# Decoder trunk on one core: another order of steps in the two MLPs

## The chip, the cores and the metric

The kernel runs on one core of one Trainium2 chip. The metric is the device time in microseconds of one execution, and the median of several runs is compared. TensorE is called PE below, VectorE DVE, ScalarE ACT, GpSimd POOL, and SyncE SP, as the profile names them.

## What is computed

The reference is a causal decoder trunk of two layers on 256 tokens with a width of 2048, all in float32. Each layer adds an attention mixer and then a dense MLP with a hidden width of 8192. The change touches the MLPs alone:

```python
for layer in range(DEPTH):                       # 2 layers
    h = rmsnorm(x, ln_mix[layer])
    x = x + (even_mixer if layer % 2 == 0 else odd_mixer)(h, ...)
    h = rmsnorm(x, ln_mlp[layer])
    x = x + jnp.square(jax.nn.relu(h @ w1)) @ w2  # w1 2048x8192, w2 8192x2048
return rmsnorm(x, ln_final)
```

## The kernel before

Everything in float32 is made of two halves in PE's float32r type: a high half (a cast by ACT, `wh`) and a low half (what the cast left, a subtraction by DVE, `wl`), and a product takes two or three matmuls of halves. `split` (L149 to L151) makes one pair.

The work of an MLP is one list of steps, `order`, written by the kernel itself and kept as it stands on every engine (the scheduler is off in there). The hidden width is cut into 16 units of 512 columns, and the units into six chunks of 2, 3, 3, 3, 3 and 2 units.

- An **up step** (class `Up`) multiplies two 128-row blocks of `w1` with the transposed input. Eight of them make a unit in four PSUM banks; at the last, `leave` (L746) takes the banks out: four copies by ACT, four additions by DVE, then Relu and Square by ACT. There are four such banks in all, so the next unit's first step needs the additions done. Later `build` turns a unit into the halves that the down steps read: `ah` (ACT) and `al` (DVE) of its values, and of four differences.
- A **down step** multiplies a unit with rows of `w2`. In chunks 0 to 4 two kinds alternate: `Seven` (L848) does a 2x2 block product in seven products instead of eight, for which DVE first adds up four sums `T` (three additions, `sums`) and then ACT and DVE split the weights and the sums into `sh` and `sl` (`split`); `Eight` is the plain product. At a block's last step, `Eight.end` puts the results together (six DVE operations) and queues two additions into `x`. The last chunk has plain steps only.
- `downs(c)` gives a chunk's down steps in four blocks of 512 output columns; `woven` (L960) puts the up steps of chunk c+1 between the down steps of chunk c.
- Most halves are made by ACT and DVE, but some up steps are "moved" (`Up.early`, L785): ACT casts the high half `mh` and writes its negative to `ml`, and a DMA issued by POOL adds the raw weights to `ml` on the way, so that DVE does nothing for them. Here these are the steps i = 1, 4 and 7 of a unit's eight.

Step names used from here on: U2.1.7 is the up step i = 7 of unit 1 of chunk 2, and a star marks a moved one (U2.1.7*); S1.b2.0 and E1.b2.1 are the Seven and the Eight at places 0 and 1 of block 2 of chunk 1's down steps; P5.b0.0 is a plain one of the last chunk.

The loop over the list (L1017) sets how far ahead each engine's part stands in that engine's queue. At place p it emits, in this order: the load for p+7 (SP; six raw buffers), `split` for p+2, `early` for p+4, `sums` for p+3, then the matmuls of p, what ends it (`leave` or `Eight.end`), and one piece of the queue `later` (parts of `build`, additions into `x`):

```python
for p in range(-7, len(order)):
    at(p + 7).load()
    at(p + 2).split()
    at(p + 4).early()
    at(p + 3).sums()
    ...
    at(p).product()
    at(p).end()
    queue_units(p + 1)
    if later:
        later.popleft()[1]()
```

Between the first chunk's up steps and the rest stands one call, `begin` (L976): it ends the input's norm (thirteen small DVE operations) and builds both units of chunk 0 at once.

Of the kernel before, what the change touches and what calls it, by code (L numbers as in the profile page):

```python
# [23 lines left out]
KT = D // P  # L24
# [42 lines left out]
def decoder_trunk(ctx, tc, const, x_in, ln_mix, ln_mlp, ln_final, e_w_in, e_g_q, e_g_kv, e_w_uq, e_w_ukv, e_w_out,  # L67
# [52 lines left out]
    def tick(rate=1):  # L120
        for _ in range(min(rate, len(pend))):
            pend.popleft()()
# [4 lines left out]
    def flush():  # L127
        tick(len(pend))
# [150 lines left out]
    def finish_norm(ss):  # L279
        tot = small.tile([P, NT], F32, name=nm("tot"), tag="tot", bufs=2)  # L280
        r = small.tile([P, NT], F32, name=nm("r"))
        nc.vector.tensor_reduce(tot, ss, axis=AX.X, op=ALU.add)
        rsqrt(r, tot, NT, D)
        return r
# [425 lines left out]
    def mlp(layer, ss, done, tail=None):  # L710
# [3 lines left out]
        with ExitStack() as st:  # L714
# [228 lines left out]
            units = [[Unit(c, n) for n in range(m)] for c, m in enumerate(CHUNKS)]  # L943
            last = len(CHUNKS) - 1

            def ups(c, moved):
                return [Up(u, i, moved and i % 3 == 1) for u in units[c] for i in range(KT // 2)]

            def downs(c):


                seq = []
                for n in range(4):
                    block = {}
                    cs = slice(n * 512, n * 512 + 512)
                    seq.append([Eight(block, i, units[c], cs, c, False) if i % 2 else Seven(block, i, units[c], cs, c)
                                for i in range(2 * CHUNKS[c])])
                return seq

            def woven(a, blocks):  # L960

                out, n = [], len(blocks)
                for j, b in enumerate(blocks):
                    part = a[len(a) * j // n : len(a) * (j + 1) // n]
                    rest, i = part[2:], 0
                    out += part[:2]
                    for k, s in enumerate(b):
                        out.append(s)
                        while i < len(rest) and i * len(b) < (k + 1) * len(rest):
                            out.append(rest[i])  # L970
                            i += 1
                return out

            order = ups(0, False)

            def begin():  # L976
                flush()
                r = finish_norm(ss)
                nc.vector.tensor_mul(rr, r, r)
                for u in units[0]:  # L980
                    u.ready = False
                    for part in u.build():
                        part()

            order.append(Call(begin))
            for c in range(last):
                order += woven(ups(c + 1, True), downs(c))
            blocks = [slice(n * 512, n * 512 + 512) for n in range(4)]
            if tail:
                blocks[3] = slice(1536, 1792)  # L990
# [5 lines left out]

            def queue_units(p):

                for c in range(1, last + 1):
                    for u in units[c]:  # L1000
                        if u.ready and p >= free[c - 1].get(u.n, 0):
                            u.ready = False
                            later.extend((u, part) for part in u.build())


            free, use = [{} for _ in CHUNKS], {}
            for p, s in enumerate(order):
                if isinstance(s, (Plain, Seven)):
                    u = s.units[s.i // 2]
# [3 lines left out]
            if tail:  # L1013
                cs, k0 = slice(1792, 2048), 4 * sum(CHUNKS[:last])
                ends = [Last(j, k0 + 4 * j, cs, j % 2 == 0) for j in range(CHUNKS[last])]
                order += ends
            for p in range(-7, len(order)):  # L1017
                at = lambda q: order[q] if 0 <= q < len(order) else Call(None)
                at(p + 7).load()
                at(p + 2).split()  # L1020
                at(p + 4).early()
                at(p + 3).sums()
                if p < 0:
                    continue
                while p in need and any(u is need[p] for u, _ in later):
# [6 lines that stand above are left out]
                tick()  # L1032
# [10 lines left out]
    ss = even_mixer(new_ss())  # L1043
    ss2 = new_ss()
    mlp(0, ss, lambda n, cs: pend.extend(norm_block(1, n, ss2)))
    ss = odd_mixer(ss2)

# [22 lines left out]
    def leave(t, cs):  # L1070
# [14 lines left out]
        for h in range(0, D, 512):  # L1085
            nc.sync.dma_start(ov[t][:, h : h + 512], xt[:, h : h + 512])

    mlp(1, ss, both, leave)


# [25 lines left out]
```

## Time and profile before

| what | us |
|---|---|
| median of 3 runs (lowest to highest) | 2281.58 (2280.48 to 2284.74) |
| the profiled execution's own time | 2283.93 |
| its span, first to last instruction | 2282.2 |
| PE busy in that span | 2216.2 (97%) |
| DVE busy | 1601.7 (70%) |
| ACT busy | 1245.5 (55%) |
| the two MLPs in the span | 399.8 to 1142 and 1533 to 2263 |

All durations come from the profiled execution. Its PE waits are listed by what released them, and its timeline gives each instruction's start, its length and the idle time before it.

### The profile page before, as it was taken

The page shows a single profiled execution, that of the slowest core. Times are in us where ns is not written, and L with a number is a line of the kernel's source. Part 1 is how long each engine was busy: PE and PEld are TensorE (multiplying, and loading weights), DVE is VectorE, ACT ScalarE, POOL GpSimd, SP SyncE. Part 2 cuts the span into 40 slices and gives each one's busy share as a digit, 9 for nine tenths or more (in the row PEclk, how much of TensorE's full clock was granted, in tenths as well). Part 3 has the DMA queues.
Part 4 walks back from the last instruction along what each step waited for, and adds up shares of the span by engine and source line. Part 5 has one row for each costly group of instructions (what it writes and reads, how often), then busy time and mean ns, then how long its engine had stood idle before and what let it go on. Part 6 is the DMA issues. An engine that isn't in the chain of part 4 may idle for free.

```text
span 2282.2 us, 33668 instructions
## 1 busy us (share of the span) xinstructions
PE 2216.2 (97%) x13086; PEld 1947.4 (85%) x13086; DVE 1601.7 (70%) x2481; ACT 1245.5 (55%) x1659; POOL 72.6 (3%) x88
## 2 busy tenths in 40 slices
PE   8999999999999999999999999998999999999998
PEld 7899988788888888888799999887888888888886
DVE  6767655566778787787665566556667777876786
ACT  6454545555656556555544444455556565556553
POOL 0000000000000000000000000000000000000000
PEclk9999999999999999999999999999999999999999
DMA  7655545578777778677565555455878777786764
GB/s 246 177 164 148 158 157 172 169 219 230 216 205 227 217 219 237 204 216 221 165 192 168 172 170 175 166 175 164 232 213 235 209 223 219 212 250 192 222 203 148
DMA packets 225692, 451.42 MB, mean 198 GB/s; under 512 B 16182, under 2 KB 21244, under 8 KB 225532
## 3 DMA queue, kind: packets, MB, share of 16 engines
q1 hardware_dynamic: 213436, 405.23, 55.8%
q0 software_dynamic: 12096, 44.05, 10.7%
q8 instruction: 102, 1.67, 0.3%
q14 instruction: 58, 0.48, 0.1%
HBM read 403.08 MB, written 2.10 MB: 178 GB/s over the span
## 4 chain that ended last, share of the span: by engine, by line
PE 75%; DVE 10%; issue 6%; DMA 6%; ACT 3%; SPq 0%; DVEq 0%; POOLq 0%
PE bank L185 17%; PE bank L186 16%; PE bank L184 16%; PE bank L809 14%; PE bank L810 7%; DMA ml<-raw 3%; DVE wl L151 3%; DMA raw<-in_mlp_w_dram 2%; DVE sl L151 2%; PE pt L223 1%; ACT wh L150 1%; PE ps L445 1%; DVE x L914 1%; DVE al L151 1%; ACT ah L150 1%
## 5 line engine op out<-in xcount | busy, mean ns | idle before, releaser
L151 DVE TENSOR_TENSOR wl<-raw,wh 128x1024 fp32r<-128x1024 f32 (+3 forms) x554 | 665.7, 1211 | 389.1 <-ACT wh L150 381.1
L150 ACT CAST wh<-raw 128x1024 fp32r<-128x1024 f32 (+3 forms) x554 | 568.6, 1037 | 387.8 <-PE bank L186 162.8
L809 PE MATMUL bank<-xx,wh 128*128 128x512 f32 x1376 | 493.1, 398 | 6.6 <-DVE a L751 6.6
L810 PE MATMUL bank<-xx,wl 128*128 128x256 f32 x1376 | 387.6, 282 | 0.0
L809 PEld LDWEIGHTS bank<-xx,wh 128*128 128x128 f32 x1376 | 260.1, 189 | 67.3 <-DVE a L751 7.6
L810 PEld LDWEIGHTS bank<-xx,wl 128*128 128x128 f32 x1376 | 260.8, 190 | 4.0 <-DVE wl L151 1.6
L184 PE MATMUL bank<-sh,ah 128*128 128x256 f32 (+1 forms) x856 | 250.2, 292 | 13.6 <-ACT sh L150 13.6
L185 PE MATMUL bank<-sl,ah 128*128 128x256 f32 (+1 forms) x856 | 251.7, 294 | 8.4 <-DVE sl L151 8.0
L150 ACT CAST sh<-T 128x1024 fp32r<-128x1024 f32 x112 | 117.8, 1052 | 241.4 <-DVE T L867 241.1
L186 PE MATMUL bank<-sh,al 128*128 128x256 f32 (+1 forms) x856 | 249.4, 291 | 0.0
L809 PE MATMUL bank<-xx,mh 128*128 128x512 f32 x672 | 243.4, 398 | 0.0
L185 PE MATMUL bank<-xx,wh 128*128 128x256 f32 x768 | 216.5, 282 | 0.0
L184 PE MATMUL bank<-xx,wh 128*128 128x256 f32 x768 | 216.3, 282 | 0.0
L186 PE MATMUL bank<-xx,wl 128*128 128x256 f32 x768 | 215.6, 282 | 0.0
L810 PE MATMUL bank<-xx,ml 128*128 128x256 f32 x672 | 192.4, 286 | 17.0 <-DMA ml<-raw 16.9
L185 PE MATMUL bank<-wl,ah 128*128 128x512 f32 (+1 forms) x520 | 204.6, 393 | 1.4 <-DVE wl L151 1.4
L184 PE MATMUL bank<-wh,ah 128*128 128x512 f32 (+1 forms) x520 | 204.4, 393 | 0.0
L186 PE MATMUL bank<-wh,al 128*128 128x512 f32 (+1 forms) x520 | 203.5, 391 | 0.0
L184 PEld LDWEIGHTS bank<-sh,ah 128*128 128x128 f32 x856 | 164.8, 193 | 22.1 <-ACT sh L150 14.8
L185 PEld LDWEIGHTS bank<-sl,ah 128*128 128x128 f32 x856 | 164.6, 192 | 15.8 <-DVE sl L151 13.4
L186 PEld LDWEIGHTS bank<-sh,al 128*128 128x128 f32 x856 | 165.0, 193 | 2.2
L809 PEld LDWEIGHTS bank<-xx,mh 128*128 128x128 f32 x672 | 127.8, 190 | 28.5
(192 smaller groups left out, 3899.1 us busy)
## 6 DMA issues: line engine op xcount, KB each, us to landing
raw<-in_mlp_w_dram SPq DMA_DIRECT2D x510, 512.0 KB, 4.9
raw<-in_o_w_in_dram SPq DMA_DIRECT2D x96, 512.0 KB, 4.1
ml<-raw POOLq DMA_DIRECT2D x84, 512.0 KB, 7.0
raw<-in_e_w_in_dram SPq DMA_DIRECT2D x71, 512.0 KB, 3.6
raw<-in_e_w_out_dram SPq DMA_DIRECT2D x32, 512.0 KB, 3.6
raw<-in_o_w_out_dram SPq DMA_DIRECT2D x32, 512.0 KB, 3.6
raw<-in_e_w_uq_dram SPq DMA_DIRECT2D x8, 384.0 KB, 3.2
raw<-in_e_w_in_dram SPq DMA_DIRECT2D x8, 320.0 KB, 3.9
```

The costliest lines, as they stand in the source:

```text
L150: nc.scalar.copy(hi, raw)
L151: on.tensor_tensor(lo, raw, hi.bitcast(F32), op=ALU.subtract)
L184: nc.tensor.matmul(o, ah, bh, start=first, stop=False, **kw)
L185: nc.tensor.matmul(o, ah, bl, start=False, stop=False, **kw)
L186: nc.tensor.matmul(o, al, bh, start=False, stop=last, **kw)
L223: nc.tensor.transpose(o, src, ident[: src.shape[0], : src.shape[0]])
L445: nc.tensor.matmul(o, q[:, h, t * P : t * P + P], k[:, h, : SPAN[t][1]], start=True, stop=True)
L809: nc.tensor.matmul(u.o[f], wh[:, kk, fs], xx[:, k], start=k == 0, stop=False, skip_group_check=True)
L810: nc.tensor.matmul(u.o[f][:, 0, :], wl[:, kk, fs], xx[:, k, 0], start=False, stop=k == KT - 1, skip_group_check=True)
L914: nc.vector.scalar_tensor_tensor(x[:, t, cs], o, rr[:, t : t + 1], x[:, t, cs], op0=ALU.mult, op1=ALU.add)
```

## The change

It does four things. (1) `begin` is moved four up steps on: the list now goes from the first chunk straight to U1.0.0, U1.0.1, U1.0.2*, then `begin`, U1.0.3 and only then S0.b0.0; `begin` no longer builds the units, which go through the queue `later` like all others. (2) In `woven`, where a unit's first step would stand after a single down step, it is swapped with the next down step, so that two down steps stand between units; it looks only within one chunk's weave. (3) The halves of a Seven are emitted three places ahead instead of two, and the sums four instead of three; `early` comes ahead of the splits. (4) Moved are the steps i = 2 and 5 of eight, instead of 1, 4 and 7: 56 transfers by POOL instead of 84.

```diff
--- before.py
+++ after.py
@@ -944,7 +944,7 @@
             last = len(CHUNKS) - 1
 
             def ups(c, moved):
-                return [Up(u, i, moved and i % 3 == 1) for u in units[c] for i in range(KT // 2)]
+                return [Up(u, i, moved and i % 3 == 2) for u in units[c] for i in range(KT // 2)]
 
             def downs(c):
 
@@ -957,18 +957,23 @@
                                 for i in range(2 * CHUNKS[c])])
                 return seq
 
-            def woven(a, blocks):
+            def woven(a, blocks, lead=2):
 
                 out, n = [], len(blocks)
                 for j, b in enumerate(blocks):
                     part = a[len(a) * j // n : len(a) * (j + 1) // n]
-                    rest, i = part[2:], 0
-                    out += part[:2]
+                    rest, i = part[lead:], 0
+                    out += part[:lead]
+                    lead = 2
                     for k, s in enumerate(b):
                         out.append(s)
                         while i < len(rest) and i * len(b) < (k + 1) * len(rest):
                             out.append(rest[i])
                             i += 1
+
+                for k in range(2, len(out) - 1):
+                    if isinstance(out[k], Up) and out[k].i == 0 and isinstance(out[k - 2], Up) and not isinstance(out[k + 1], Up):
+                        out[k : k + 2] = out[k + 1], out[k]
                 return out
 
             order = ups(0, False)
@@ -977,14 +982,10 @@
                 flush()
                 r = finish_norm(ss)
                 nc.vector.tensor_mul(rr, r, r)
-                for u in units[0]:
-                    u.ready = False
-                    for part in u.build():
-                        part()
-
-            order.append(Call(begin))
+
             for c in range(last):
-                order += woven(ups(c + 1, True), downs(c))
+                order += woven(ups(c + 1, True), downs(c), 2 if c else 4)
+            order.insert(len(units[0]) * KT // 2 + 3, Call(begin))
             blocks = [slice(n * 512, n * 512 + 512) for n in range(4)]
             if tail:
                 blocks[3] = slice(1536, 1792)
@@ -996,9 +997,9 @@
 
             def queue_units(p):
 
-                for c in range(1, last + 1):
+                for c in range(last + 1):
                     for u in units[c]:
-                        if u.ready and p >= free[c - 1].get(u.n, 0):
+                        if u.ready and p >= (free[c - 1].get(u.n, 0) if c else 0):
                             u.ready = False
                             later.extend((u, part) for part in u.build())
 
@@ -1014,12 +1015,14 @@
                 cs, k0 = slice(1792, 2048), 4 * sum(CHUNKS[:last])
                 ends = [Last(j, k0 + 4 * j, cs, j % 2 == 0) for j in range(CHUNKS[last])]
                 order += ends
-            for p in range(-7, len(order)):
+            for p in range(-8, len(order)):
                 at = lambda q: order[q] if 0 <= q < len(order) else Call(None)
                 at(p + 7).load()
-                at(p + 2).split()
                 at(p + 4).early()
-                at(p + 3).sums()
+                for ahead in (2, 3):
+                    if isinstance(at(p + ahead), Seven) == (ahead == 3):
+                        at(p + ahead).split()
+                at(p + 4).sums()
                 if p < 0:
                     continue
                 while p in need and any(u is need[p] for u, _ in later):
```

What this does to the queues at three places follows; the numbers behind a name tell buffers apart.

The first is ACT's queue at `begin` of the first MLP. Ahead of it stand the four copies of unit U0.1 (`a_795` before, `a_800` now); `a_767` is U0.0. Before:

```order
L752 ACTIVATE a_795_4380<-a_795_4380 128x1024
L753 ACTIVATE a_795_4380<-a_795_4380 128x1024
L150 CAST ah_803_4416<-a_767_4190 128x1024
L150 CAST ah_803_4416<-s_805_4420 128x512
L150 CAST ah_806_4426<-a_795_4380 128x1024
L150 CAST ah_806_4426<-s_808_4430 128x512
L150 CAST sh_810_4438<-raw_783_4291 128x768
L150 CAST sh_810_4438<-T_797_4393 128x1024
```

And now:

```order
L752 ACTIVATE a_800_4394<-a_800_4394 128x1024
L753 ACTIVATE a_800_4394<-a_800_4394 128x1024
L150 CAST ah_801_4405<-a_800_4394 128x1024
L150 CAST ah_801_4405<-s_808_4431 128x512
L150 CAST wh_812_4461<-raw_789_4323 128x1024
L150 CAST sh_814_4465<-raw_792_4345 128x768
L150 CAST sh_814_4465<-T_810_4435 128x1024
L150 CAST wh_823_4510<-raw_797_4372 128x1024
```

U0.0 is built eight steps earlier now; only U0.1 is left, and between its second cast and the halves of S0.b0.0 (`sh_814`) stands the high half of U1.0.3 (`wh_812`).

The second is DVE's queue at the passage from chunk 1 to chunk 2, that is from U1.2.7 to U2.0.0, behind the last combination of E0.b3.3 (L909, L914). Before:

```order
L909 TENSOR_TENSOR v_974_5452<-bank_949_5279,v_974_5452 128x512
L914 SCALAR_TENSOR_TENSOR x_74<-v_974_5452,rr_725_3969,x_74 128x512
L865 TENSOR_TENSOR T_977_5464<-raw_959_5351 128x512
L866 TENSOR_TENSOR T_977_5464<-T_977_5464,raw_959_5351 128x256
L867 TENSOR_TENSOR T_977_5464<-T_977_5464,raw_959_5351 128x256
L751 TENSOR_TENSOR a_978_5484<-bank_924_5148,a_978_5484 128x256
```

And now:

```order
L909 TENSOR_TENSOR v_973_5448<-bank_952_5285,v_973_5448 128x512
L914 SCALAR_TENSOR_TENSOR x_74<-v_973_5448,rr_725_3969,x_74 128x512
L151 TENSOR_TENSOR wl_979_5466<-raw_956_5331,wh_978_5465 128x1024
L151 TENSOR_TENSOR sl_981_5470<-raw_959_5349,sh_980_5469 128x768
L151 TENSOR_TENSOR sl_981_5470<-T_972_5432,sh_980_5469 128x1024
L751 TENSOR_TENSOR a_982_5491<-bank_930_5178,a_982_5491 128x256
```

Ahead of U1.2's additions (L751) stood the three sums of S1.b0.0; now these stand ahead of the combination, and the low half of U2.0.1 (`wl_979`) and both low halves of S1.b0.0 (`sl_981`) have come in their place.

The third is ACT's queue at the passage from chunk 2 to chunk 3, behind the last copy of unit U2.2. Before:

```order
L752 ACTIVATE a_1181_6750<-a_1181_6750 128x1024
L753 ACTIVATE a_1181_6750<-a_1181_6750 128x1024
L903 COPY v_1184_6779<-bank_1143_6509 128x256
L150 CAST sh_1187_6791<-raw_1166_6648 128x768
L150 CAST sh_1187_6791<-T_1183_6763 128x1024
```

And now:

```order
L752 ACTIVATE a_1180_6743<-a_1180_6743 128x1024
L753 ACTIVATE a_1180_6743<-a_1180_6743 128x1024
L789 CAST mh_1182_6756<-raw_1169_6662 128x1024
L790 ACTIVATE ml_1183_6757<-mh_1182_6756 128x1024
L150 CAST wh_1184_6761<-raw_1161_6607 128x1024
```

The two operations for U3.0.2* (`mh_1182`, `ml_1183`) now stand behind Relu and Square of U2.2, and the high half of U3.0.1 (`wh_1184`), which was a moved step before, stands behind them; the matmuls of U3.0.1 come two places later in PE's queue than those of E1.b3.5, with U3.0.0 between.

## Rows read from the trace of the kernel before

**Rows 1.** Page, part 1: busy time and share of the span, by engine.
```profile
PE 2216.2 (97%) x13086; PEld 1947.4 (85%) x13086; DVE 1601.7 (70%) x2481; ACT 1245.5 (55%) x1659; POOL 72.6 (3%) x88
```

**Rows 2.** Waits of PE: line <- releaser: us in total, times, longest us.
```profile
PE bank L810 <- DMA ml<-raw: 16.9, 13, 2.3
PE bank L184 <- ACT sh L150: 13.6, 2, 6.8
PE bank L185 <- DVE sl L151: 8.0, 16, 1.0
PE bank L809 <- DVE a L751: 6.6, 2, 3.3
...
PE bank L185 <- DVE wl L151: 1.9, 6, 0.5
```

**Rows 3.** Timeline, PE at `begin`: start us, us, engine, line, operation [idle before].
```profile
448.48 0.39 PE L809 MATMUL bank<-xx,mh 128*128 128x512 f32 x1
...
458.25 0.58 PE L184 MATMUL bank<-sh,ah 128*128 128x256 f32 x1 [6.78 <-ACT sh L150]
...
463.91 0.39 PE L809 MATMUL bank<-xx,wh 128*128 128x512 f32 x1
```

**Rows 4.** Timeline, ACT and then DVE at `begin`.
```profile
448.78 1.03 ACT L150 CAST ah<-a 128x1024 fp32r<-128x1024 f32 x1
453.00 0.62 ACT L150 CAST ah<-s 128x512 fp32r<-128x512 f32 x1 [3.19 <-DVE s L770]
...
460.32 3.49 DVE L151 TENSOR_TENSOR wl<-raw,wh 128x1024 fp32r<-128x1024 f32 x3
463.73 0.69 DVE L865 TENSOR_TENSOR T<-raw 128x512 f32<-128x512 f32 x1
...
465.25 0.95 DVE L151 TENSOR_TENSOR sl<-raw,sh 128x768 fp32r<-128x768 f32 x1
```

**Rows 5.** Timeline, PE and DVE at the passage from U1.2.7* to U2.0.0.
```profile
569.33 0.79 PE L809 MATMUL bank<-xx,wh 128*128 128x512 f32 x1 [3.32 <-DVE a L751]
573.75 0.40 PE L809 MATMUL bank<-xx,mh 128*128 128x512 f32 x1
...
568.86 1.41 DVE L751 TENSOR_TENSOR a<-bank,a 128x256 f32<-128x256 f32 x4
```

**Rows 6.** Timeline, PE, DVE and ACT at the passage from U2.2.7* to U3.0.1*.
```profile
704.84 0.39 PE L809 MATMUL bank<-xx,wh 128*128 128x512 f32 x1
707.64 0.39 PE L809 MATMUL bank<-xx,mh 128*128 128x512 f32 x1
709.44 0.39 PE L810 MATMUL bank<-xx,ml 128*128 128x256 f32 x1 [1.41 <-DMA ml<-raw]
...
686.89 1.23 DVE L151 TENSOR_TENSOR al<-a,ah 128x1024 fp32r<-128x1024 f32 x1 [4.24 <-ACT ah L150]
...
702.29 1.41 DVE L751 TENSOR_TENSOR a<-bank,a 128x256 f32<-128x256 f32 x4
...
703.74 1.06 ACT L752 ACTIVATE a<-a 128x1024 f32<-128x1024 f32 x1 [1.12 <-DVE a L751]
```

**Rows 7.** Timeline, PE and ACT after U2.1.7*, whose last matmul is the row before 653.57.
```profile
653.57 0.28 PE L184 MATMUL bank<-sh,ah 128*128 128x256 f32 x1
...
656.08 0.39 PE L184 MATMUL bank<-wh,ah 128*128 128x512 f32 x1
...
654.63 1.06 ACT L752 ACTIVATE a<-a 128x1024 f32<-128x1024 f32 x1 [0.49 <-DVE a L751]
...
659.67 0.81 ACT L150 CAST sh<-raw 128x768 fp32r<-128x768 f32 x1
```

**Rows 8.** Stretches: us, busy by engine, PEclk (granted clock), DMA share, GB/s.
```profile
979.34:981.50 2.16, 0.38 (x3) 0.07 (x1) 2.06 (x5) 2.16 (x4) 0.00 (x0) 1.00 0.86 283
981.54:985.70 4.16, 4.16 (x15) 3.56 (x16) 4.16 (x6) 1.55 (x2) 0.00 (x0) 0.59 0.74 235
```

**Rows 9.** Tile `ml`: from issue to landing of its 84 transfers.
```profile
DMA to landing us min/median/max: 4.8/7.0/11.2
```

## The prediction

> **What bounds the kernel now.** The page's first part comes first: PE is busy for 2216.2 us, 97% of the span [rows 1]. The change adds no matmul and takes none away; it only puts them in another order. So the time can only move by what PE waits for and by its clock. The second view is PE's list of waits [rows 2]: transfers into `ml` 16.9 us in 13 waits, ACT's `sh` 13.6 in 2, DVE's `sl` 8.0 in 16, DVE's `a` (the banks of a unit not yet taken out) 6.6 in 2, DVE's `wl` 1.9 in 6. All lie in the two MLPs, which repeat each other place by place; together 47.0. Two things add to it. An idle is counted from a matmul's modelled end: in U3.0.1* the second matmul starts 1.80 after the first [rows 6], where it is free to start after 0.23 (an up step of 2.80 us is eight pairs of 512 and 256 columns, so 0.35 a pair and two thirds of it for the first); that is 1.57 lost for an idle of 1.41, 0.16 more, and 6 for the 39 waits. And after the longer waits PE goes on at half its clock: S0.b0.0 takes 463.91 - 458.25 = 5.66 us [rows 3], against 2.51 for S1.b2.2 [rows 7], of which 0.6 are two of the `sl` waits and 2.5 the clock; U2.0.0 takes 4.42 against 2.80, so 1.6 [rows 5]; and behind a wait that left PE 0.38 busy of 2.16 the granted clock is 0.59 of full speed for 4.16 us, so 4.16 x 0.41 = 1.7 [rows 8]. That is 5.8 an MLP, 11.6 in all. The whole of what PE loses in the MLPs is then 47 + 6 + 12 = 65 us. This is all that an order can win; of it one `sl` wait per MLP of 1.0, in the last chunk, is at a place that the change leaves as it is. What may vanish or come back is 63.
>
> **At `begin`.** U1.0.1* begins at 448.48 and is done 2.80 later, at 451.28; S0.b0.0 begins at 458.25 [rows 3]. These 7.0 and the 3.1 of the slow step are 10.1 an MLP. Now U0.0 is built eight steps earlier, beside up steps in which ACT and DVE have room, and PE has U1.0.2* and U1.0.3 to do, until 456.9. But U1.0.3 has to be halved, and its high half stands behind U0.1's second cast on ACT (first order rows). Step by step: `ah` ends at 449.81 [rows 4]; DVE makes `al` (1.14: three low halves in a row take 463.73 - 460.32 = 3.41), the sums `s` (half as many columns as `T`, which takes 465.25 - 463.73 = 1.52; so about 0.9 with their starts) and `T`, until 453.4; the second cast 0.6; the high half of U1.0.3 about 1.0, until 455.1; its low half 1.14, until 456.25. U1.0.3 is due at 454.08, so its second matmul comes 456.25 - 0.23 - 454.08 = 1.9 late. The thirteen small operations of the norm come behind the halves of S0.b0.0 and delay nothing that is due. I add a fall of the clock, 1.7, because two idles of about 1.0 with one matmul between them come nearest to the 1.8 of [rows 8]. Now 3.6, before 10.1.
>
> **Where a moved step stands behind a unit's end.** After U2.1.7*, Relu starts 1.06 after the last matmul, and the fifth operation after that is under way until 659.67, 6.1 after the unit's end [rows 7]. In the changed order five such operations stand between a unit's end and the high half of an up step in two kinds of place, because the moved step is now i = 2 and its `mh` and `ml` are emitted ahead of the halves of i = 0 or 1. The first is U1.2.0, two down steps behind U1.1.7: due 2.51 + 2.80 = 5.3 after the unit's end, high half there after 6.2, low half after 7.35; 1.8 late, and 1.7 for the clock as above: 3.5, new.
>
> The second is each passage from a chunk to the next from chunk 2 on (U2.2 to U3.0, U3.2 to U4.0, U4.2 to U5.0; third order rows), and there DVE is late as well. From 686.89, where PE's freeing of `ah` lets it begin, DVE works through to the additions of U2.2 at 702.29 [rows 6]. Ahead of them there is now one low half more, U2.2.7 being no longer moved (1.14), and the sums of S2.b0.0, emitted a step earlier (1.52): 704.95. The first bank is free 0.4 later, U3.0.0 was due at 704.84: 0.5 late. Relu starts 1.45 after the additions' start, as before (703.74 against 702.29), at 706.4; the high half of U3.0.1 ends 5.1 later, 711.5, the low half at 712.7; its second matmul was due at 705.35 + 2.80 + 0.23 = 708.4: 4.3 late. With the clock, 1.7, this is 6.5 a passage, 19.5 an MLP. Before, a passage lost a wait for `ml` of 1.4 to 2.3 [rows 2, 6].
>
> **At the first passage,** U1.2.7 to U2.0.0, the swap of (2) does not reach: the two steps stand in different weaves, and still side by side. The additions of U1.2 start at 568.86 because the combination of E0.b3.3 and three sums stand ahead of them, and U2.0.0 waits until 569.33 [rows 5]. The sums go (1.52), `wl` of U2.0.1 and both `sl` of S1.b0.0 come (1.14 + 0.95 + 1.14, second order rows): 1.7 later; and since the sums now stand ahead of the combination, that starts up to 0.4 later too. So 3.5 + 2.1 = 5.6, and for the clock 2.0, between the 1.6 after an idle of 3.3 and the 2.5 after 6.8: 7.6; before 5.1.
>
> **Inside a chunk** (after U2.1.7 and its like in three chunks) the waits for `sl` and `ml` go: only one high half and the `sh` pair stand behind Square now, U2.2.1 is halved 4 us ahead of its use, and U2.2.2* has its transfer issued some 8 us ahead, against 7.0 in the median [rows 9]. I count nothing there, and 0.9 at E4.b2.1, whose low half falls behind a combination and three sums (3.1 + 1.3 + 1.5 of DVE work under two steps). Of the 28 transfers less, ACT loses 28 casts and DVE gains 28 subtractions (28 x 1.14 = 32 us over both MLPs): paid where it stands in the sums above, elsewhere covered by the 30% of the span in which DVE is free [rows 1].
>
> **A transfer's price** decides how much more can come. On the rows, `ml` lands 4.8 to 11.2 us after its issue. At a passage it is now issued at about 711 and needed at about 719.4: 7.0 is in time, 11.2 would be 2.8 late. I take the median, so nothing. The Trainium skill, in "DMA: Bandwidth & Descriptors", section "Anatomy of one DMA — SWDGE (gpsimd) path", fits 2.0 us plus the bytes at 436 GB/s, an estimate of 3.2 us for these 512 KB: by that no `ml` would ever be late and the sum would stay as it is. The smallest landing here is 4.8, so the trace does not agree, and the rows decide.
>
> **The sum.** New: 3.6 + 3.5 + 7.6 + 19.5 + 0.9 = 35.1 an MLP, 70 in both, against 63 that go: 7 us slower. The profiled execution took 2283.93 (span 2282.2), so 2291 like it; it lies 2.4 above the median of the runs, and against that median I say 2289.
>
> **Rivals.**
> - *The passages cost no more than U1.2.0.* If DVE catches up ahead of them (its row at 686.89 had been idle for 4.24), the additions start with the unit's end, and a passage costs 1.8, at full clock or not: 3 x 4.7 less an MLP, 28 in all, so 2261. It decides at one point: whether U2.2's additions end before about 703 instead of 706.4. For it: a shift of ACT's or DVE's start by little moves the rest. Against: from 686.89 on the list leaves DVE no gap but two of 0.7. Half of this gives 2275.
> - *The clock stays up* where I charge it for two short idles (`begin`, U1.2.0): 2 x 3.4 = 7 less, 2282, no change. The row with 1.41 idle shows a full clock, that with 1.8 a fall; mine lie at the edge.
> - *Transfers land late*, as at U3.0.1* before (about 10 us after issue): 1.7 at each passage and about 2 after each unit inside a chunk, 11 an MLP: 2311. Three loads at a time ran there; fewer transfers in all speak against it.
> - *The change does less than it says:* this is so for the swap at the passages, seen in the order, and is in the sum.
>
> Chances: the forecast 0.37 (its own range 2283 to 2296), passages cheap 0.24, clock up 0.25, transfers late 0.14. A measurement of this kernel can tell 0.2%, 4.6 us, from no change. Faster 0.25, within 0.28, slower 0.47. The range takes in half of the cheap passages and half of the late transfers: 2264 to 2303.
>
> **What would show it.** Right: PE's waits for `sh` gone (13.6), a wait of about 1.0 before `wh` and `wl` in U1.0.3, `a` waits up from 6.6 to some 14 in 8 places, and `wh` (ACT) waits of about 3.3 in six places, at U3.0.1, U4.0.1 and U5.0.1; granted clock below 0.7 behind these. Wrong: additions of U2.2 that end within 1.5 us of U2.2.7's last matmul, or `ml` waits that remain above 5 us in all.

## The result and the profile after

| what | before | the change |
|---|---|---|
| median, us | 2281.03 (4 runs, 2280.20 to 2284.74) | 2297.01 (4 runs, 2294.80 to 2298.64) |
| ratio, 95% interval | | 1.0066 (1.0049 to 1.0084) |
| the profiled execution's own time, and its span | 2283.93, 2282.2 | 2297.91, 2296.1 |
| mean granted clock of the profiled execution | 0.993 | 0.987 |

The change is slower, by 16 us between the medians and 11 to 19 by the interval. The forecast was 2289 and slower, with a range from 2264 to 2303. Part 1 of the page after, to be held against [rows 1]:

```profile
PE 2230.3 (97%) x13086; PEld 1957.1 (85%) x13086; DVE 1629.7 (71%) x2509; ACT 1215.9 (53%) x1631; POOL 48.5 (2%) x60
```

PE runs the same 13086 matmuls and is busy 14.1 us longer (2230.3 against 2216.2), in a span that is 13.9 longer. PE's waits after say what that means:

```profile
PE bank L809 <- ACT wh L150: 21.7, 10, 3.1
PE bank L809 <- DVE a L751: 13.8, 8, 5.3
PE bank L810 <- DVE wl L151: 8.5, 12, 0.8
...
PE bank L185 <- DVE sl L151: 1.9, 2, 0.9
...
PE bank L185 <- DVE wl L151: 0.7, 3, 0.3
PE bank L810 <- DMA ml<-raw: 0.6, 1, 0.6
```

They come to 47.2 us in 36 waits, against 47.0 in 39 in [rows 2]. The change has not lengthened PE's idle: it took away the waits for `sh` and nearly all those for `ml` and `sl`, and put waits for `wh`, `a` and `wl` of the same sum in their place. But after the new waits PE goes on at half its clock more often. In the MLPs before, the granted clock is 0.50 in six stretches (`begin`, U2.0.0 and U5.0.1* of each), with 22.9 us of matmuls in them; after, in eleven (U1.0.3, U2.0.0, U3.0.1, U4.0.1 and U5.0.1 of each, and U1.2.0 of the first), with 48.6. Matmuls take twice as long there (0.79 us against 0.40 in [rows 5]), so half of that time is lost, and half of the difference is 12.9 of the 14.1 us: nearly the whole loss is slower matmuls.

A table by place follows. A step's loss is the time from its first matmul's start to the next step's, less 2.81 us for an up step, 2.80 for an Eight and 2.52 for a Seven, the lengths of undisturbed ones; a wait ahead of a step's first matmul counts with the step before. Only losses over 0.15 are summed, and the first two steps of each MLP (0.8) and its last chunk, the same in both kernels, are left out. Both MLPs together:

| place | before | after |
|---|---|---|
| `begin` (U1.0.1 to S0.b0.0) | 20.2 | 7.5, and 1.8 at U0.1.2 |
| U1.2.0 | 0 | 5.6 |
| first passage, U1.2.7 to U2.0.0 | 10.2 | 15.9 and 0.3 |
| the three other passages | 13.8 | 42.6 |
| inside chunks 1 to 3 | 17.4 | 1.1 |
| inside chunk 4 | 2.7 | 3.1 |
| sum | 64.3 | 77.8 |

The difference, 13.5, is nearly the span's 13.9. The change gains 27 us, 10.9 at `begin` and 16.3 inside chunks 1 to 3; the passages take back 35, U1.2.0 another 5.6.

**`begin`.** The timeline after, PE, then ACT, then DVE, beside [rows 3, 4]:

```profile
457.00 0.49 PE L809 MATMUL bank<-xx,wh 128*128 128x512 f32 x1 [0.97 <-ACT wh L150]
458.26 0.39 PE L810 MATMUL bank<-xx,wl 128*128 128x256 f32 x1 [0.77 <-DVE wl L151]
...
450.66 1.05 ACT L150 CAST ah<-a 128x1024 fp32r<-128x1024 f32 x1
455.38 0.62 ACT L150 CAST ah<-s 128x512 fp32r<-128x512 f32 x1 [3.68 <-DVE s L770]
455.91 1.04 ACT L150 CAST wh<-raw 128x1024 fp32r<-128x1024 f32 x1
...
456.98 1.23 DVE L151 TENSOR_TENSOR wl<-raw,wh 128x1024 fp32r<-128x1024 f32 x1 [0.25 <-ACT wh L150]
```

U1.0.3's high half stands behind U0.1's second cast, as the order said; the two idles are 0.97 and 0.77, and the place loses 3.8 where 10.1 were lost.

**U1.2.0 and the first passage,** PE at both and DVE at the second, beside [rows 5]:

```profile
529.15 0.50 PE L809 MATMUL bank<-xx,wh 128*128 128x512 f32 x1 [0.75 <-ACT wh L150]
530.41 0.39 PE L810 MATMUL bank<-xx,wl 128*128 128x256 f32 x1 [0.76 <-DVE wl L151]
...
570.47 0.80 PE L809 MATMUL bank<-xx,wh 128*128 128x512 f32 x1 [5.34 <-DVE a L751]
...
568.86 1.22 DVE L151 TENSOR_TENSOR sl<-T,sh 128x1024 fp32r<-128x1024 f32 x1
570.00 1.41 DVE L751 TENSOR_TENSOR a<-bank,a 128x256 f32<-128x256 f32 x4
```

U2.0.0 waits 5.34 instead of 3.32 for the additions, which stand right behind S1.b0.0's low halves.

**A passage**, U2.2.7 to U3.0.1, beside [rows 6]: PE, then DVE, then ACT.

```profile
705.00 0.50 PE L809 MATMUL bank<-xx,wh 128*128 128x512 f32 x1 [0.53 <-DVE a L751]
711.13 0.49 PE L809 MATMUL bank<-xx,wh 128*128 128x512 f32 x1 [3.05 <-ACT wh L150]
712.39 0.58 PE L810 MATMUL bank<-xx,wl 128*128 128x256 f32 x1 [0.77 <-DVE wl L151]
...
701.87 1.23 DVE L151 TENSOR_TENSOR wl<-raw,wh 128x1024 fp32r<-128x1024 f32 x1 [0.26 <-ACT wh L150]
703.01 0.68 DVE L865 TENSOR_TENSOR T<-raw 128x512 f32<-128x512 f32 x1
...
704.53 1.41 DVE L751 TENSOR_TENSOR a<-bank,a 128x256 f32<-128x256 f32 x4
...
705.98 1.06 ACT L752 ACTIVATE a<-a 128x1024 f32<-128x1024 f32 x1 [3.06 <-DVE a L751]
...
708.03 1.03 ACT L789 CAST mh<-raw 128x1024 fp32r<-128x1024 f32 x1
709.09 1.06 ACT L790 ACTIVATE ml<-mh 128x1024 fp32r<-128x1024 f32 x1
710.05 1.03 ACT L150 CAST wh<-raw 128x1024 fp32r<-128x1024 f32 x1
```

Read it from the middle: DVE makes a low half and the sums `T` before it takes unit U2.2 out at 704.53; so Relu starts at 705.98, ACT had been idle for 3.06 until then; behind Square come `mh` and `ml` of U3.0.2*, and only then the high half that U3.0.1 waits for. PE is idle 0.53, 3.05 and 0.77. The clock shows by stretch: U3.0.0 and the idle behind it, U3.0.1, and U5.0.1 of the same MLP (columns as in [rows 8]):

```profile
705.00:711.10 6.10, 3.08 (x16) 2.44 (x16) 0.94 (x3) 5.06 (x6) 0.66 (x1) 1.00 0.16 61
711.10:716.40 5.30, 4.50 (x16) 3.68 (x17) 5.12 (x8) 5.30 (x7) 0.20 (x1) 0.68 0.88 181
...
987.90:994.10 6.20, 5.33 (x16) 4.34 (x17) 5.94 (x9) 4.63 (x7) 0.28 (x1) 0.55 0.90 228
```

The clock is full up to the idle and falls when PE goes on. Transfers into `ml` land 4.5 to 6.8 us after their issue, against 4.8 to 11.2 in [rows 9]:

```profile
DMA to landing us min/median/max: 4.5/5.7/6.8
```

### The profile page after: what moved, and what is told of

The parts are those of the page before. It is cut to its first block, busy times and chain, and to the rows that moved or that the text cites. A ratio compares the mean times of both kernels' runs of the same rounds, so it can differ in the third digit from the quotient of the medians.

```text
span 2296.1 us, 33636 instructions
## 1 busy us (share of the span) xinstructions
PE 2230.3 (97%) x13086; PEld 1957.1 (85%) x13086; DVE 1629.7 (71%) x2509; ACT 1215.9 (53%) x1631; POOL 48.5 (2%) x60
## 4 chain that ended last, share of the span: by engine, by line
PE 84%; DVE 8%; ACT 4%; issue 3%; DMA 1%; SPq 0%; DVEq 0%; ACTq 0%; POOLq 0%
PE bank L185 18%; PE bank L184 18%; PE bank L186 18%; PE bank L809 17%; PE bank L810 9%; DVE wl L151 3%; DVE sl L151 1%; ACT wh L150 1%; ACT ah L150 1%; PE pt L223 1%; DVE a L751 1%; ACT a L752 1%; PE ps L445 1%; PE po L378 1%; DVE T L865 0%
## 5 line engine op out<-in xcount | busy, mean ns | idle before, releaser
L151 DVE TENSOR_TENSOR wl<-raw,wh 128x1024 fp32r<-128x1024 f32 (+2 forms) x582 | 701.2, 1212 | 424.1 <-ACT wh L150 418.1
L150 ACT CAST wh<-raw 128x1024 fp32r<-128x1024 f32 (+2 forms) x582 | 596.4, 1038 | 424.3 <-PE bank L186 159.8
L809 PE MATMUL bank<-xx,wh 128*128 128x512 f32 x1600 | 590.2, 407 | 35.5 <-ACT wh L150 21.7
L810 PE MATMUL bank<-xx,wl 128*128 128x256 f32 x1600 | 460.7, 288 | 8.5 <-DVE wl L151 8.5
L809 PEld LDWEIGHTS bank<-xx,wh 128*128 128x128 f32 x1600 | 310.3, 194 | 113.3 <-ACT wh L150 25.1
L810 PEld LDWEIGHTS bank<-xx,wl 128*128 128x128 f32 x1600 | 311.4, 195 | 19.0 <-DVE wl L151 16.6
L186 PE MATMUL bank<-xx,wl 128*128 128x256 f32 x768 | 215.6, 282 | 0.0
L809 PE MATMUL bank<-xx,mh 128*128 128x512 f32 x448 | 159.7, 394 | 0.0
L184 PEld LDWEIGHTS bank<-xx,wh 128*128 128x128 f32 x768 | 144.7, 188 | 0.5
L185 PEld LDWEIGHTS bank<-xx,wh 128*128 128x128 f32 x768 | 144.7, 188 | 0.4
```

The costliest lines, as they stand in the source:

```text
L150: nc.scalar.copy(hi, raw)
L151: on.tensor_tensor(lo, raw, hi.bitcast(F32), op=ALU.subtract)
L184: nc.tensor.matmul(o, ah, bh, start=first, stop=False, **kw)
L185: nc.tensor.matmul(o, ah, bl, start=False, stop=False, **kw)
L186: nc.tensor.matmul(o, al, bh, start=False, stop=last, **kw)
L809: nc.tensor.matmul(u.o[f], wh[:, kk, fs], xx[:, k], start=k == 0, stop=False, skip_group_check=True)
```

## The experiments

All times are medians; the runs of before that belong to each are 2281.13 (runs 1 to 4), 2282.17 (5 to 8), 2283.58 (9 and 10) and 2282.64 (11 and 12). They lie up to 2.6 apart, and the change was measured beside 2281.03, so a difference between a run and the change is uncertain by as much. "Theory A" and "Theory B" stand in the texts written ahead of each run.

**Run 1: part (1) alone.** The kernel before with these lines, and `woven` and `queue_units` as the change has them for it:

```diff
-                for u in units[0]:
-                    u.ready = False
-                    for part in u.build():
-                        part()
-            order.append(Call(begin))
+            order.insert(len(units[0]) * KT // 2 + 3, Call(begin))
```

> The kernel before with part (1) of the change alone: begin stands behind four up steps less one, and the units of chunk 0 are built through the queue. Theory A (each part is priced by its own place): the 10.1 us per MLP at begin shrink to about 3, and some 0.9 come new at U0.1.2, where U0.0 is now built beside up steps; so about 12 us faster than before, 2269, with a rest of up to 3 per MLP if the transfer for U1.0.4* lands late. Theory B (what is won at begin comes back later, because the norm's small operations and the first combinations then stand in DVE's way): within 4 us of before, with new waits in the first block of chunk 0.

2270.43, ratio 0.9950 (0.9937 to 0.9964): 10.7 us faster than before. The losses at `begin` are 4.4 per MLP (1.5 of them a late `ml` for U1.0.4*) and 0.87 at U0.1.2, so 4.8 less, 9.7 in both. Theory A. What is won there does not come back. The change without this part was not run.

**Run 2: `mh` and `ml` behind the high half.**

```diff
-                at(p + 4).early()
-                for ahead in (2, 3):
-                    if isinstance(at(p + ahead), Seven) == (ahead == 3):
-                        at(p + ahead).split()
+                if not isinstance(at(p + 2), Seven):
+                    at(p + 2).split()
+                at(p + 4).early()
+                if isinstance(at(p + 3), Seven):
+                    at(p + 3).split()
```

> The change, but the two ACT operations of a moved step (mh, ml) are emitted behind the split of an up step or Eight two places ahead, and still ahead of a Seven's. Theory A (ACT's order makes the loss at the passages): the wait for wh at U3.0.1 and its like shrinks by the 2.1 us of the two operations, from 3.05 to about 1, U1.2.0's 1.5 goes, and the clock falls less behind them; ml of U3.0.2* then lands up to 2 late. So 2284, some 13 us faster than the change, or 2273 if the transfers are in time. Theory B (DVE's late additions make the loss, and everything behind them only follows): the waits for the banks and what stands behind them stay within 0.5 us a passage, 2297.

2289.51, 7.5 faster than the change. At U3.0.1, PE's timeline:

```profile
709.77 0.50 PE L809 MATMUL bank<-xx,wh 128*128 128x512 f32 x1 [1.03 <-ACT wh L150]
711.03 0.39 PE L810 MATMUL bank<-xx,wl 128*128 128x256 f32 x1 [0.76 <-DVE wl L151]
```

The wait for `wh` shrinks by 2.02 us, the two operations. But U3.0.1 and its like still take 5.3 to 5.5 us. In four of the six places the clock falls behind the idles of 1.03 and 0.76. In the other two (U5.0.1 of the first MLP, U4.0.1 of the second) it stays at 1.00, and the time goes to idle instead, because the Seven behind waits for DVE's combination:

```profile
PE bank L184 <- DVE u L904: 2.4, 2, 1.2
```

So at full clock or not, the step behind comes no sooner: there DVE bounds the passage. A further 0.8 to 0.9 is lost at S2.b0.0 and its like, and `ml` waits of 6.1 us come back. ACT's order is a part of the loss: the six passages cost 32.5 together where the change's cost 42.6, and U1.2.0 loses nothing; but half of these 15.7 us are lost again.

**Run 3: moved steps 1, 4 and 7 again** (part (4) undone).

```diff
-                return [Up(u, i, moved and i % 3 == 2) for u in units[c] for i in range(KT // 2)]
+                return [Up(u, i, moved and i % 3 == 1) for u in units[c] for i in range(KT // 2)]
```

> The change with the moved steps of before, i = 1, 4 and 7 (part (4) undone). Theory A: U3.0.1 needs no wh again, so the six passages lose only a late transfer of 1.4 to 2.3 each instead of about 7, U1.2.0 loses nothing; mid-chunk ml waits of about 1 come back in three places per MLP, the begin gain stays; 2262. Theory B: DVE's additions are late by the sums alone, 1.5 of the 2.7 us, the clock falls as often, and the transfers are 84 again: about 2285.

2308.35, 11 slower than the change: both theories wrong. I had overlooked U2.2.0, which is now what U1.2.0 is in the change: `mh` and `ml` of U2.2.1* stand ahead of its high half behind Square of U2.1, and it waits 0.77 and 0.76 and loses 2.0 to 3.6, three times per MLP. At a passage U3.0.1* waits for nothing long, but S2.b0.0, U3.0.2, S2.b0.2 and E2.b0.3 then lose 0.9, 1.5, 0.6 and 1.1, so 6.0 in all with the 1.8 of the banks and U3.0.1*, hardly less than the change's 6.5 to 7.8. And U1.0.2 and U1.0.3 lose 6.8 to 7.7.

**Run 4: before's distances** (part (3) undone).

```diff
-                at(p + 4).early()
-                for ahead in (2, 3):
-                    if isinstance(at(p + ahead), Seven) == (ahead == 3):
-                        at(p + ahead).split()
-                at(p + 4).sums()
+                at(p + 2).split()
+                at(p + 4).early()
+                at(p + 3).sums()
```

> The change with before's distances (part (3) undone): halves of a Seven two places ahead, sums three, mh and ml behind the splits. Theory A: the additions at a passage start 1.5 us sooner and wh another 2.1 sooner, so the bank wait goes and the wh wait falls from 3.05 to under 1, but S2.b0.0's halves then stand behind mh and ml (1 to 1.5 late) and the sl wait of 0.8 in the middle of three chunks per MLP is back: 2284. Theory B: with the additions on time the whole 7 us of a passage go, 42 less and 5 back in the middle of chunks: 2260.

2304.67, 7.7 slower than the change: again neither. The wait for `wh` falls to 0.2 and the banks are in time, but the Seven behind pays:

```profile
709.81 0.53 PE L185 MATMUL bank<-sl,ah 128*128 128x256 f32 x1 [3.06 <-DVE sl L151]
...
702.51 1.23 DVE L151 TENSOR_TENSOR wl<-raw,wh 128x1024 fp32r<-128x1024 f32 x1 [3.15 <-ACT wh L150]
703.65 0.68 DVE L865 TENSOR_TENSOR T<-raw 128x512 f32<-128x512 f32 x1
...
708.81 0.95 DVE L151 TENSOR_TENSOR sl<-raw,sh 128x768 fp32r<-128x768 f32 x1
```

DVE is idle for 3.15 until U3.0.1's high half is there, makes the sums only behind its low half, and between them and S2.b0.0's low halves come a whole combination and an addition into `x`, 3.6 us. That step loses 5.0 to 5.7 us, about a third of it clock. So beside the change's other parts its distance for a Seven is worth having; this does not hold by itself, since run 11 is the fastest of all with a Seven's halves two places ahead, and run 12 with three is 21 slower. Run 11 puts the sums first in their place, ahead of that low half.

**Run 10: the sums behind the additions**, with all else as in the change.

```diff
                 at(p + 4).early()
+                at(p + 3).sums()
                 for ahead in (2, 3):
                     if isinstance(at(p + ahead), Seven) == (ahead == 3):
                         at(p + ahead).split()
-                at(p + 4).sums()
```

> The change, but a Seven's three sums are emitted three places ahead instead of four, in the place of its split and ahead of it, so that at a passage they stand behind the additions that take the unit out and not in front; mh and ml still ahead of wh. Theory A (the lateness of DVE and the order of ACT add up): the bank wait of 0.53 and its 0.7 go, Relu starts 1.5 sooner, wh at U3.0.1 1.5 sooner, the wait there 2.3 instead of 3.05 and still long enough for the clock to fall; 1.7 less at each of six passages, 2287. Rival (ACT's five operations alone decide): 2297. Rival (the passages are cheap once DVE is in time, as the prediction's first rival has it, 1.8 each): 2267.

2285.57, 11.4 faster than the change, and theory A to within 1.5 us. (Beside its own runs of before it is 2.0 slower, where the change is 16.0 slower; so counted, it gains 14.) PE at U3.0.1, and DVE's additions:

```profile
707.37 0.49 PE L809 MATMUL bank<-xx,wh 128*128 128x512 f32 x1 [2.32 <-ACT wh L150]
...
700.77 1.41 DVE L751 TENSOR_TENSOR a<-bank,a 128x256 f32<-128x256 f32 x4
```

The bank wait is gone and the passage costs 4.2 to 6.0 instead of 6.5 to 7.8. So DVE's sums are a part of the loss, ACT's order another, and the time of a passage is not 1.8 once the sums alone are out of the way.

**Run 7: no swap** (part (2) undone): the three lines behind `woven`'s loop are left out.

> The change without the swap of a unit's first step with the next down step (part (2) undone). Theory A: U1.2.0's high half then stands ahead of U1.1.7's end on ACT, so its 3.6 and 2.1 us go and nothing comes at U1.2.1, whose high half is needed 8 us after the unit's end: 2291, 6 us faster than the change. Rival: U1.2.0 then waits 2 to 3 us for the banks that are not yet taken out, at full or half clock, because only one down step of 2.5 us stands between: 2297 or slower.

2297.72, the change's time. U1.2.0 is rid of its wait, and the step behind it, E0.b2.3, takes it over (0.75 and 0.76 in the change):

```profile
527.98 0.51 PE L184 MATMUL bank<-wh,ah 128*128 128x512 f32 x1 [0.74 <-ACT wh L150]
529.24 0.50 PE L185 MATMUL bank<-wl,ah 128*128 128x512 f32 x1 [0.76 <-DVE wl L151]
```

Whatever step comes third behind the unit's end needs the first high half that ACT makes after it. In the change the swap is worth nothing.

**Run 6: the clock's price.** Before U3.0.1, U4.0.1 and U5.0.1 the change gets twelve matmuls of zeros into the unit's first bank (`zero` is a tile of zeros, made once at the start of the kernel; its lines are not shown):

```diff
+                    if i == 1 and u.n == 0 and u.c > 2:
+                        for _ in range(12):
+                            nc.tensor.matmul(u.o[0], zero, xx[:, 0], start=False, stop=False, skip_group_check=True)
```

> The change with twelve matmuls of a zero weight tile ahead of U3.0.1, U4.0.1 and U5.0.1; they add zeros to the unit's first bank while PE would wait for wh. Nothing is left out. Twelve of 0.235 us are 2.8 of the 3.05 us idle. Theory A (a third of the change's loss is the clock that falls behind these idles): U3.0.1 then takes 2.8 plus the 0.8 wait for wl instead of 5.3 to 6.1, granted clock stays near 1, 2 us less at each of six passages, 2285. Rival: the clock falls with what ACT and DVE do there or with any kind of wait, not with PE's idle: 2297 or, with the filler's own time, up to 2300.

2292.00, 5 faster than the change, with 72 more matmuls. The stretch of U5.0.1, against 6.20 us and 0.55 above:

```profile
985.07:989.01 3.94, 3.18 (x16) 2.55 (x17) 3.91 (x5) 3.94 (x6) 0.17 (x1) 1.00 0.84 153
```

All six steps take 3.94 to 3.95 us, each at a granted clock of 1.00, against 5.3 to 6.1 in the change, so it was PE's idle that let the clock fall there, and not what ACT and DVE do meanwhile. The steps of the six passages are 8.1 us shorter together, the span 6.7. The 12 written down were too many because U3.0.1 and its like still wait 0.25 to 0.30 and 0.76 for their halves and S2.b0.0 and its like, reached sooner, lose 0.6 for theirs where the change lost 0 to 0.5.

**Run 5: moved steps 0, 3 and 6**, whose `mh` and `ml` stand ahead of a unit's end.

```diff
-                return [Up(u, i, moved and i % 3 == 2) for u in units[c] for i in range(KT // 2)]
+                return [Up(u, i, moved and i % 3 == 0) for u in units[c] for i in range(KT // 2)]
```

> The change with the steps i = 0, 3 and 6 moved instead of 2 and 5, all else as in the change. No moved step's mh and ml then stand on ACT between a unit's end and the first high half of the next unit that needs one. Theory A (the loss sits in what ACT has to do between a unit's Square and the next high half): the wh waits at U1.2.0 (1.5) and at the six passages (3.05) go or fall below 1, the bank wait at a passage shrinks by the 1.14 of U3.0.0's low half, and the clock falls less there: 7 a passage becomes about 2, so 5 x 6 + 5 = 35 less, 2262; the begin part may lose about 3 per MLP to a late transfer for U1.0.3. Theory B (any queue order hands the same lateness to the next step, since ACT has the same work behind a unit's end): the waits move to S2.b0.0 and U3.0.2 and the time stays within 10 us of 2297.

2273.15, 24 faster than the change and 9 faster than before (ratio 0.9961, 0.9948 to 0.9973). U1.2.0 loses nothing; a passage 4.3: 1.05, 1.15, 0.6 and 1.5, on U3.0.0*, U3.0.1, S2.b0.0 and U3.0.2. Theory A has the direction and two thirds of the size, theory B the 1.5 at U3.0.2.

**Runs 8, 9, 11 and 12: towards a faster order.** All have part (1), no swap, and the moved steps 0, 3 and 6 (2 and 5 in unit U1.0). Run 11's loop is

```diff
+                at(p + 3).sums()
                 at(p + 2).split()
                 at(p + 4).early()
-                at(p + 3).sums()
```

against before. Run 8 has besides a down step between U1.2.7 and U2.0.0 (`order[k - 2 : k] = order[k - 1], order[k - 2]`). Run 9 is run 8 with a Seven's `split` three places ahead, and with a unit queued for `build` after the place's piece of `later` is taken. Run 12 is run 11 with a Seven's `split` three places ahead, behind the sums and ahead of `early`.

> A version from the readings so far: begin later as in part (1), no swap inside a weave, distances as before (Sevens two ahead, sums three, the sums first in the place), moved steps i = 0, 3 and 6 (2 and 5 in unit U1.0), and the last down step of chunk 0 put behind U1.2.7 so that a down step of 2.8 us stands between it and U2.0.0. Theory A, place by place per MLP: U0.1.2 0.9, begin 3.0, the first passage 1 instead of 5.1, the three other passages about 1.5 each, the middle of chunks 0, the last chunks 2 to 4: about 13 against 32 before, so 38 less than before, 2243. Theory B (the lateness is handed on): no better than part (1) alone, 2270.

> The candidate before with two more edits: a Seven's halves three places ahead again, behind its sums of the same place, so that its low halves stand ahead of the combination of the Eight before it; and a finished unit's build is put into the queue after the place's piece of work is taken, so that its halves come one place later, behind the next high half. Theory A: the 2.6 us at S2.b0.0, S3.b0.0 and S4.b0.0 shrink to about 0.5 (then its banks, not its halves, come last), U0.1.2's 0.85 goes, U2.0.1 and S1.b0.0 together lose 2 to 3 instead of 5 to 6: some 10 per MLP less, 2245. Theory B (the work behind a unit's end is the same and the next reader pays): 2260 or more.

> The first candidate without the down step put between U1.2.7 and U2.0.0. Theory A (the down step between them bought the bank wait with a longer queue of halves: there U2.0.1, S1.b0.0, U2.0.2, U2.0.3 and S1.b0.2 lost 8.7 us per MLP): the bank wait of 3.3 with its slow step, 5 to 6 per MLP, is back and the 8.7 go; about 3 per MLP less, 2259. Rival (the queue of halves behind U1.2.7 is late with or without it): both are lost, 2272.

> The same as the run without the down step at U2.0.0, but with a Seven's halves three places ahead, behind its sums, so that they stand ahead of the combination of the Eight before it. Theory A (what bounds a passage is DVE's total work in it, about as long as PE's): the 2.55 us at S2.b0.0 and its like fall to 0.6, but U3.0.1 waits some 1 for its low half behind the sums and U3.0.2 1.5 for its own behind the combination, so the time stays within 4 us of the run without this edit, on either side. Theory B (it is the place of the halves ahead of the combination alone): 2 less at six passages, 12 us faster, 2248.

| run | us | what decided |
|---|---|---|
| 8 | 2264.62 | the bank wait at U2.0.0 gone, but 8.8 and 8.7 lost from U2.0.1 to S1.b0.2 |
| 9 | 2294.04 | S1.b0.2 waits 6.9 for `ah`, built a place later: 9.9 per MLP; `ml` waits of 14.4 |
| 11 | 2255.24, ratio 0.9881 (0.9868 to 0.9893) | 27 faster than before, the best of all |
| 12 | 2276.72 | `ml` waits of 14.4, bank waits of 7.3 |

Run 8 gained half of what had been written down (2243). For run 9 2245 had been written down, and it came out 10 slower than its runs of before. Run 11 came out below its 2259. Its waits:

```profile
PE bank L185 <- DVE sl L151: 14.2, 14, 1.5
PE bank L810 <- DVE wl L151: 4.8, 6, 1.6
PE bank L810 <- DMA ml<-raw: 4.5, 4, 2.1
...
PE bank L809 <- DVE a L751: 3.3, 2, 1.6
```

Its passages lose 2.6 each (3.9 and 4.1 in two where the clock falls), nearly all at the Seven, whose low halves stand behind a combination. Run 12 set out to win these 2.6: the passages then lose 2.6 to 2.7 in other places (0.6, 0.6 and 1.5, at U3.0.1, S2.b0.0 and U3.0.2), as theory A has it. Its extra 21 us come from elsewhere. At the first passage it loses 5.4 per MLP where run 11 loses 1.8: both `sl` of S1.b0.0 again stand ahead of U1.2's additions on DVE. And the waits for `ml` rise from 4.5 to 14.4, because a Seven's second cast now waits on ACT for sums that DVE has not made yet, and a moved step's operations wait behind it; this was followed at U1.0.5*, and U2.1.3* has the like (2.11 for the sums). PE and ACT at U1.0.5*:

```profile
474.32 0.58 PE L810 MATMUL bank<-xx,ml 128*128 128x256 f32 x1 [3.41 <-DMA ml<-raw]
...
464.01 1.05 ACT L150 CAST sh<-T 128x1024 fp32r<-128x1024 f32 x1 [4.79 <-DVE T L867]
464.97 1.04 ACT L789 CAST mh<-raw 128x1024 fp32r<-128x1024 f32 x1
466.04 1.06 ACT L790 ACTIVATE ml<-mh 128x1024 fp32r<-128x1024 f32 x1
```

No text had that. Runs 2 and 10 were not put together, nor run 10 with run 5; what they would give was not tried.

## Why the prediction was right

The direction, and the mechanism at each place, were those forecast. The direction owes something to luck: it was the difference of 7 us between sums of 70 and 63, slower had been given 0.47, and the errors of the sum happened to lie on its side. 2297 lies in the range and 1 above the forecast's own, 2283 to 2296. Point by point:

- **What may vanish:** 63 us, counted from waits, their correction and the clock; by steps 64.3 were lost before, and they are gone or newly made.
- **`begin`:** 3.6 per MLP, measured 3.8. Run 1 shows the part by itself. The wait of "about 1.0 before `wh` and `wl`" is 0.97 and 0.77.
- **U1.2.0:** 3.5; measured 3.6 in the first MLP and 2.0 in the second. The idle is 1.51 in both; in the second the clock did not fall. So the rival with the clock up is right in one place of four, where its condition was said to lie at the edge.
- **First passage:** 7.6; measured 7.9 and 8.0, with `wl` and both `sl` ahead of the additions.
- **The other passages:** 6.5 each; measured 6.5, 7.2, 7.8 and 6.7, 7.7, 6.7. Relu was expected at 706.4 and starts at 705.98, the high half's end at 711.5 and comes at 711.08, the low half's at 712.7 and comes at 712.3; the unit ends 0.5 sooner than before (701.50), so against its end all three are 0.1 late. Its additions start 3.0 after that end and end 4.4 after it, so the sign against (within 1.5) did not come. Runs 2 and 10 show the two causes apart: without ACT's two operations in front the time falls by 7.5 us, with DVE's sums behind the additions by 11.4 to 14; the six passages alone cost 10.1 and 12.1 less.
- **Inside the chunks:** nothing was counted in chunks 1 to 3, and 1.1 are left of 17.4. In chunk 4, 0.9 was charged at E4.b2.1, which loses 0.2 to 0.3. The waits for `ml` are 0.6 in all, so late transfers, the fourth case, did not come; but that fewer transfers speak against them is not borne out (run 3, last section).
- **The sign on the markers:** `a` waits 13.8 in 8 places (14 in 8 expected), `wh` waits of about 3.05 at the six passages (3.3), granted clock 0.68 and 0.55 behind them.

The step that was off is the sum: new losses of 70 us, measured 77.8, so 7 slower where the profile has 13.5 and the medians 16. Mis-sized were the passages, by 3.6 over six: U3.0.1's second matmul comes at 712.39 where 707.34 would be free of waits, so 5.05 late (4.8 forecast), and what is left of the six losses, 2.05 on average, is mostly clock, where 1.7 was charged by a wait half as long [rows 8]. Over all places the clock was charged with 21.0; PE's 48.6 us at half clock make it 24.3. Left out were U0.1.2 (1.8: U0.0's low half now stands ahead of U0.1.2's on DVE), small waits behind the first passage and in the chunks (1.6) and E4's low halves in chunk 4 of the second MLP (1.0). The first passage and `begin` were 1.0 dearer, U1.2.0 1.4 cheaper.

The rival that ended faster said that a passage costs 1.8 once DVE is in time. Its condition did not come, and no run with the change's moved steps brings it about: in run 10 a low half still stands ahead of the additions, which start 1.5 after the unit's last matmul, and the passage costs 4.2 to 6.0. In run 11, with other moved steps, they start with the unit's end, and a passage costs 2.6 to 4.1.

## What to carry to other kernels

Behind the end of a unit several engines have a fixed bundle of work to do, and moving one piece of it hands its lateness to the next reader (runs 3, 4, 7 and 12 each undid one wait and met it again a step later); what helped was to let pieces fall due ahead of that end (run 11) or to start a long fixed part elsewhere (run 1). Where the idle sum of the bottleneck engine does not change, look at where the idles lie and at what the engine does behind them: the same 47 us cost 14 more, because PE went on at half its clock in eleven places instead of six. And undo each part of a change by itself, but not only so: of this one's four parts the first gave 10.7 alone and the second nothing, while undoing the third alone cost 7.7 and the fourth alone 11. One would call both good. Yet run 1, which has neither (nor the swap), is 27 faster than the change: each of the two repairs a part of what the other does, and together they lose, the third by the order of three lines in a place (runs 2 and 10).

## What the chip showed that was not expected

- **The same idle, two clocks.** U1.2.0 of the change waits 0.75 and 0.76 in both MLPs and loses 2.7 in one and 1.1 in the other; in run 5, U3.0.1 and its like idle 1.63 to 1.66 six times and take 3.9 to 4.0 four times and 5.5 twice. U1.2.0's idle of 1.51 is the same in runs 10 and 6, and the clock falls behind it in both MLPs of run 10 (2.7 lost) and in neither of run 6 (1.15 lost). So one number for the price of a short idle does not fit these runs. The Trainium skill, "TensorE: Matmul & The Clock Gate", section "Part 1: The HAM clock gate (the "warmup" mystery)", says that the count of slow matmuls differs between runs of one kernel; here it differs between like places of one execution as well.
- **Zeros keep the clock up.** Twelve matmuls of a zero weight tile in the idle held the granted clock at 1.00 where it was 0.55 to 0.68 without.
- **The number of transfers does not say how soon they land.** With 56 accumulating transfers instead of 84, the median from issue to landing fell from 7.0 to 5.7 us and the longest from 11.2 to 6.8. But run 3 has 84 with a median of 5.3 and at most 9.0, and runs 2 and 4 have 56 with medians of 6.3 and 6.2 and at most 9.0 and 8.7. What sets it stays open. By the Trainium skill's fit, "DMA: Bandwidth & Descriptors", section "Anatomy of one DMA — SWDGE (gpsimd) path", each would take 3.2 us, an estimate for 512 KB; no landing in these runs is under 4.5.
